# Mixing projection of a hybrid decoder layer: split weights and merged rows through DRAM, row form, first up pair from split units

## The chip, the cores and the metric

One NeuronCore of one Trainium2 chip runs the whole layer in one launch. The metric is the device time in microseconds (us), the median over the runs; one further execution was recorded by the profiler. Engines: TensorE (PE, matmuls), the scalar engine (ACT), the vector engine (DVE), GpSimd (POOL), and SyncE (SP), which here issues every DMA.

## What is computed

The layer takes 1024 prompt tokens and 8 sample tokens (1032 columns in all), width 1024, in float32. Cut to what matters here:

```python
z = x @ w_in                                  # bg, cg, xv, q, k, v, og, ig, fg, ga, gb
ya = (bg * causal_dwconv3(cg * xv)) @ w_proj_a
yb = (sigmoid(og) * MHLN(mlstm(q, k, v))) @ w_proj_b        # 4 heads of 256
merged = sigmoid(ga) * ya + sigmoid(gb) * yb
x = layer_norm(alpha * x + merged @ w_mix_out)              # w_mix_out: 1024 x 1024
ffn = (silu(g) * u) @ w_ffn_down,  [g, u] = causal_dwconv3(x @ w_ffn_up)   # 5632 columns
x = layer_norm(alpha * x + ffn)
```

It also returns the conv and mLSTM states and the rows of the two conv caches.

## The kernel before

Every float32 operand is split into a high and a low part (`split_unit`, `Operands.split`: a cast on ACT, L131 and L159, then a subtraction on DVE, L132 and L160), and each product is three matmuls: high by high, high by low, low by high. Operands of activations stand in SBUF as T00 to T16; split weights rotate through the slots of `WS` (the tiles WS_split, at times also RA and RB); weights are loaded as raw slabs of 1 MB into two halves of `WRB` (WR_raw in the profile).

A `pair` (L186 on) makes 256 output columns for all tokens by seven products instead of eight (combinations of the four quarters of the weight slab, made on DVE in the raw slab and in `XS`, against combinations of operands). `u` = 0 is the first half of the tokens (256 columns a matmul), `u` = 1 the second with the samples (260). Each product is 12 matmuls for each `u`; products go in the order 0 to 6, both `u` after each other, and sums are made by ACT copies into `MC` (L204) and DVE additions (L200).

The order of the program is:

1. Operands of x, then four mLSTM heads (about 140 to 640 us): pairs for K, Q, V, the head's chunks, and gate pairs (`gate_pair`: a pair, a sigmoid on ACT, the rows stored to `sg_d`) as filling, `FILL` = (1,4), (2,5), (3,6), (7,8,9).
2. The conv branch with the decode of the samples beside it (about 640 to 740), drained inside `conv_branch`; gate pair 10 (L666) into RA and RB; `cops`, the conv operands (L743 to L749), by way of `hm_d`; gate pair 11 (L750).
3. Projection A (L763 to L773, about 740 to 813): for each of 8 row blocks a gate row is loaded, 36 matmuls of 344 columns, a DVE product, a store to `ya_d`. After every second block `hidden` (L755 on) loads a piece of the head rows from `hm_d` and makes a piece of the operands `XH`.
4. Four pairs with w_proj_b (L783 to L799): yb times its gate plus ya, the merged row stored to `mg_d`. Rows, gates and ya stand in two sets of tiles in turn.
5. The mix (about 896 to 1000): `merged` loads and splits columns of `mg_d`; `mix` (L801) makes 384 and then 392 token columns, with w_mix loaded and split anew each time; `gemm_rows` (L812) makes the last 256 tokens as rows, with w_mix loaded a third time. `norm1` (L853) transposes the columns back (L863), loads the residual, adds and normalises; `back1` (L872) applies it (L877), transposes (L881), scales (L887) and stores to `x1_d`; `X1` are the operands of the up projection, made by `Operands.first` and `.second`, in which DVE combines (L173 to L179) and splits.
6. 22 up pairs (about 1046 to 1485), the down projection and the last norm.

All is placed on the engines at build time by the framework's scheduler, which fixes the order on each engine; each engine, and SP's queue of DMA issues, works in that order. `tc.issue_after` adds constraints to it.

Of the kernel before, what the change touches and what calls it, by code (L numbers as in the profile page):

```python
# [42 lines left out]
def trunk_kernel(  # L43
# [142 lines left out]
    def pair(w, X, dst, order=nullcontext(), order0=nullcontext()):  # L186
# [28 lines left out]
        with order:  # L215
            vec.tensor_tensor(S3, A11, A21, op=ALU.subtract)  # L216
# [7 lines left out]
            prod(s, 3, qq, True)  # L224
            s = split_unit(S3)
# [7 lines left out]
            vec.tensor_tensor(A12, A12, A11, op=ALU.subtract)  # L233
            s = split_unit(A12)
# [82 lines left out]
    mg_d = dram.tile([8, P, TOK], F32, name="mg_d")  # L317
# [107 lines left out]
    def gate_pair(i, rows):  # L425

        col = (COL_OG, COL_GA, COL_GB)[i // 4] + (i % 4) * 256
        pair(load_pair(w_in[0], col), X, rows_dst(*rows))
# [3 lines left out]
        for j, r in enumerate(rows):  # L432
            sp.dma_start(sg_d[2 * i + j], r)

    def conv_branch(beside):
# [24 lines left out]
        for _ in beside:  # L460
            pass
# [108 lines left out]
    FILL = ((1, 4), (2, 5), (3, 6), (7, 8, 9))  # L570
    for h in range(H):
# [3 lines left out]
        for a, col in ((1, COL_K), (0, COL_Q), (2, COL_V)):  # L575
            pair(load_pair(w_in[0], col + h * 256), X, rows_dst(*qkv[a]))
# [4 lines left out]
        if h == 0:  # L581
# [14 lines left out]
    def decode():  # L596

        vb = Blk("TMF", "dec").v3(0, NS, 256)
# [9 lines left out]
        for h in range(H):  # L608
            if h > 0:
                yield  # L610
# [4 lines left out]
            sp.dma_start(vb, vw_d[h].partition_broadcast(P))  # L615
# [17 lines left out]
            for half in range(2):  # L633
                for c in range(4):
# [89 lines left out]
    MRG = [("T00", "T01", "T02", "T03"), ("T10", "T11", "T12", "T13"), ("T14", "T15")]  # L724

# [5 lines left out]
    def merged(c, stages):  # L731

        n, span = CH[c]
        mg = Many(MRG[c], f"mg{c}", 8, n)
        for i, (k, cnt_) in enumerate(mg.parts(0, 8, 2)):
            blk, base = stages[i % len(stages)]
            a = blk.v3(base, cnt_, n)
            load_cols(a, mg_d[k:k + cnt_], span)
            mg.put(k, a)
        return mg  # L740
# [4 lines left out]
    for k in range(4):  # L745
        r = TS.v(0, TOK)
        sp.dma_start(r, hm_d[8 + k])
        for c, (lo, n) in enumerate(CA):
            cops[c].put(k, r[:, lo:lo + n].unsqueeze(1))  # L749
    gate_pair(11, SG)  # L750

# [370 lines left out]
```

## Time and profile before

| | |
|---|---|
| median of 3 runs | 1761.27 us (1755.98 to 1764.26) |
| profiled execution, its own time | 1759.24 us |
| its span (first to last instruction) | 1757.3 us, mean granted clock 0.982 |
| PE, DVE, ACT, POOL busy | 1693.0, 1234.1, 833.5, 46.8 us |
| chain that ended last | PE 87%, DVE 5%, DMA 5%, ACT 1% |
| moved by DMA | 240.03 MB, mean 137 GB/s |

PE is the engine that the others serve, so the questions are where it does not work, what released it then, and at which clock it worked. The stretches give busy time of each engine in a window and the clock that was granted (PEclk, a share of 2.4 GHz; 0.50 is 1.2 GHz). The waits add up idle time of one engine by what ended it. The chain goes back from the last instruction to whatever released each piece.

### The profile page before, as it was taken

The numbers are of one execution on the slowest core, as the hardware profiler recorded it, in microseconds if no ns is written. First come the engines' busy times: TensorE is split into PE (matmuls) and PEld (weight loads), VectorE is DVE, ScalarE is ACT, GpSimd is POOL, SyncE is SP. The second block draws the span as 40 slices with busy tenths as digits, with TensorE's granted clock in tenths as the row PEclk, the third lists the DMA queues.
The fourth block names the chain that finished last, engine by engine and source line by source line (L and its number), as shares of the span: only waits on it lengthen the run. The fifth ranks groups of instructions, "written<-read, shape, count | busy, mean of one in ns | idle before, by whom it ended". The sixth has DMA issues, their size and how long they took to land.

```text
span 1757.3 us, 32559 instructions
## 1 busy us (share of the span) xinstructions
PE 1693.0 (96%) x12793; PEld 1621.4 (92%) x12793; DVE 1234.1 (70%) x2490; ACT 833.5 (47%) x1640; POOL 46.8 (3%) x97
## 2 busy tenths in 40 slices
PE   8999999999999999997989859999999999999998
PEld 6999999999999999997989749999999999888986
DVE  8867567567477788675764668877888778645675
ACT  7545435345354544442345665544544446433442
POOL 0000001001000000000000000000000000000000
PEclk9999999999999999998999969999999999999999
DMA  4224213224224565586565631332222323845763
GB/s 153 61 83 126 91 61 108 80 67 130 76 76 145 185 204 183 181 276 242 194 224 187 195 100 61 102 104 73 73 73 84 97 74 127 271 144 173 242 210 126
DMA packets 234004, 240.03 MB, mean 137 GB/s; under 512 B 19499, under 2 KB 209979, under 8 KB 233331
## 3 DMA queue, kind: packets, MB, share of 16 engines
q1 hardware_dynamic: 233851, 237.96, 41.9%
q8 instruction: 100, 1.64, 0.4%
q14 instruction: 53, 0.43, 0.1%
HBM read 180.48 MB, written 57.54 MB: 135 GB/s over the span
## 4 chain that ended last, share of the span: by engine, by line
PE 87%; DVE 5%; DMA 5%; ACT 1%; issue 1%; SPq 0%; POOL 0%; DVEq 0%; POOLq 0%; ACTq 0%
PE wp L142 35%; PE wq L142 27%; PE wq L715 2%; PE wq L716 2%; PE wq L717 2%; PE wp L715 2%; PE wp L717 2%; PE wp L716 2%; PE wp L819 2%; PE wq L819 2%; PE pa L540 1%; PE pa L548 1%; DMA MC_copies<-hm_d 1%; PE pa L515 1%; PE pa L646 1%
## 5 line engine op out<-in xcount | busy, mean ns | idle before, releaser
L142 PE MATMUL wp<-T_x,WS_split 128*128 128x260 f32 (+2 forms) x5016 | 668.9, 285 | 4.7 <-ACT T_x L159 3.2
L142 PEld LDWEIGHTS wp<-T_x,WS_split 128*128 128x128 f32 (+1 forms) x5016 | 624.5, 188 | 15.1 <-issue 5.7
L142 PE MATMUL wq<-T_x,WS_split 128*128 128x260 f32 (+3 forms) x3792 | 504.3, 283 | 2.4 <-ACT T_x L159 0.7
L131 ACT CAST WS_split<-WR_raw 128x512 fp32r<-128x512 f32 x486 | 294.6, 612 | 443.6 <-PE wp L142 182.8
L132 DVE TENSOR_TENSOR WS_split<-WR_raw,WS_split 128x512 fp32r<-128x512 f32 x486 | 327.4, 679 | 247.3 <-ACT WS_split L131 243.5
L142 PEld LDWEIGHTS wq<-T_x,WS_split 128*128 128x128 f32 (+1 forms) x3792 | 471.6, 187 | 6.8 <-ACT T_x L159 0.9
L204 ACT COPY MC_copies<-wp 128x256 f32<-128x256 f32 (+1 forms) x336 | 123.8, 369 | 110.3 <-PE wp L142 104.7
L142 PE MATMUL wp<-T_hid,WS_split 128*128 128x260 f32 (+1 forms) x384 | 51.0, 287 | 10.9 <-DVE RA_ga L772 10.9
L132 DVE TENSOR_TENSOR WS_split<-XS_combo,WS_split 128x512 fp32r<-128x512 f32 (+1 forms) x58 | 38.9, 671 | 31.9 <-ACT WS_split L131 31.8
L142 PEld LDWEIGHTS wp<-T_hid,WS_split 128*128 128x128 f32 x384 | 48.6, 193 | 11.4 <-ACT T_hid L159 11.1
L131 ACT CAST WS_split<-XS_combo 128x512 fp32r<-128x512 f32 (+1 forms) x58 | 35.1, 608 | 37.2 <-PE wp L142 37.2
L716 PE MATMUL wp<-T_h,WS_split 128*128 128x512 f32 (+1 forms) x116 | 43.0, 371 | 0.0
L717 PE MATMUL wp<-T_h,WS_split 128*128 128x512 f32 (+1 forms) x116 | 43.0, 370 | 0.0
L715 PE MATMUL wp<-T_h,WS_split 128*128 128x512 f32 (+1 forms) x116 | 42.9, 370 | 0.0
L717 PE MATMUL wq<-T_h,WS_split 128*128 128x512 f32 (+1 forms) x116 | 42.9, 370 | 0.0
L716 PE MATMUL wq<-T_h,WS_split 128*128 128x512 f32 (+1 forms) x116 | 42.9, 369 | 0.0
L715 PE MATMUL wq<-T_h,WS_split 128*128 128x512 f32 (+1 forms) x116 | 42.8, 369 | 0.0
L216 DVE TENSOR_TENSOR XS_combo<-WR_raw 128x512 f32<-128x512 f32 x56 | 38.3, 684 | 1.6 <-DMA WR_raw<-in_w_proj_b_dram 1.0
L218 DVE TENSOR_TENSOR WR_raw<-WR_raw 128x512 f32<-128x512 f32 x56 | 38.5, 688 | 1.2
L842 POOL TENSOR_TENSOR rs<-rs,FX_fixed 128x1 f32<-128x1 f32 (+1 forms) x18 | 12.0, 668 | 1017.5 <-DVE rs L841 1017.5
L142 PE MATMUL wq<-T_hid,WS_split 128*128 128x256 f32 (+1 forms) x288 | 38.8, 287 | 0.0
L217 DVE TENSOR_TENSOR WR_raw<-WR_raw 128x512 f32<-128x512 f32 x56 | 38.3, 683 | 0.3
(528 smaller groups left out, 2628.9 us busy)
## 6 DMA issues: line engine op xcount, KB each, us to landing
WR_raw<-in_w_ffn_down_dram SPq DMA_DIRECT2D x27, 1024.0 KB
WR_raw<-in_w_in_dram SPq DMA_DIRECT2D x26, 1024.0 KB
WR_raw<-in_w_ffn_up_dram SPq DMA_DIRECT2D x44, 512.0 KB
WR_raw<-in_w_mix_out_dram SPq DMA_DIRECT2D x12, 1024.0 KB
sg_d<-RA_sg SPq DMA_DIRECT2D x12, 516.0 KB
sg_d<-RB_sg SPq DMA_DIRECT2D x12, 516.0 KB
WR_raw<-in_w_ffn_down_dram SPq DMA_DIRECT2D x8, 768.0 KB
h_d<-QA_xf SPq DMA_DIRECT2D x11, 516.0 KB
```

The costliest lines, as they stand in the source:

```text
L131: act.copy(wh, w)
L132: vec.tensor_tensor(wl, w, wh.bitcast(F32), op=ALU.subtract)
L142: pe.matmul(ps, a[:, k, :], b[:, k, :], start=start and k == 0 and i == 0, stop=stop and k == kt - 1 and i == 2, skip_group_check=onto)
L204: act.copy(t[u], ps[u][:, :UN[u]])
L216: vec.tensor_tensor(S3, A11, A21, op=ALU.subtract)
L217: vec.tensor_tensor(A21, A21, A22, op=ALU.add)
L218: vec.tensor_tensor(A11, A21, A11, op=ALU.subtract)
L515: pe.matmul(s[:, :L], kr[j][:, cs], qr[j][:, cs], start=(j == 0), stop=(j == 1))
L715: pe.matmul(ps, wh[:, i, :], xh[:, 0, :], start=s, stop=False)
L716: pe.matmul(ps, wh[:, i, :], xl[:, 0, :], start=False, stop=False)
L717: pe.matmul(ps, wl[:, i, :], xh[:, 0, :], start=False, stop=e)
L819: pe.matmul(ps[t][g], a[:, 0, cols], b[:, 0, :], start=s and i == 0, stop=e and i == 2)
```

## The change

- **Splitting ahead.** While heads 1 to 3 run, `presplit` loads w_mix and the first up pair's weights, splits them on ACT and DVE (by way of RA and RB), and stores high and low parts to DRAM (`wm_d`, `wu_d`). Three steps of it stand in each K, Q and V pair (`next(beside)`).
- **Gates and decode.** Gate pair 7 leaves head 3 and comes after gate pair 11, its rows kept in SBUF; gate pair 10 writes to QA and comes before decode is drained. Decode steps are halved.
- **Projection A.** The four pieces of `hidden` come before it; it starts with the blocks 6 and 7, whose ya stay in SBUF.
- **w_pb pairs.** Order 2, 0, 1, 3; one set of gates in QA; the merged rows are split here and both parts are stored.
- **Mix.** The split w_mix is loaded once and stays. Tiles 0 to 3, 6 and 7 of 128 tokens are made as rows (`rows_mm`), tokens 512 to 767 and the samples as columns. Residuals are loaded before they are wanted.
- **First up pair.** `first_pair` takes its seven units from `wu_d`, and goes through products 0 and 1 for both halves, then 2 to 6 for the first half, then for the second.

```diff
@@ pair: the same three steps in each K, Q, V pair of heads 1 to 3
         with order:
+            next(beside, None)
             vec.tensor_tensor(S3, A11, A21, op=ALU.subtract)
...
@@ beside the heads
+    def presplit(jobs):
+        RAW, PRE = Blk("RA", "praw"), Blk("RB", "pre", F32R)
+        def split(w, dsts):
+            h, l = (PRE.v3(i * 512, w.shape[1], w.shape[2]) for i in range(2))
+            act.copy(h, w)
+            vec.tensor_tensor(l, w, h.bitcast(F32), op=ALU.subtract)
+            for d, t in zip(dsts, (h, l)):
+                sp.dma_start(d, t.bitcast(F32))
...
+    JOBS = [()] + [[mix_job(k) for k in range(4)], [mix_job(k) for k in range(4, 8)], [up_job]]
+    FILL = ((1, 4), (2, 5), (3, 6), (8, 9))
@@ conv branch, decode, gates
-    conv_branch(decode())
+    dec = decode()
+    conv_branch(dec)
+    SQ = Blk("QA", "sg")
+    SQ = [SQ.v(i * TOK, TOK) for i in range(2)]
+    gate_pair(10, SQ)
+    for _ in dec:
+        pass
     SG = [Blk(q, "sg").v(0, TOK) for q in ("RA", "RB")]
-    gate_pair(10, SG)
...
+    gate_pair(11, SG, w=wg)
+    gate_pair(7, SG, keep=True)
@@ projection A
+    T5 = Blk("T05", "stage")
+    hidden(1, 0, P, T5.v3(0, 8, P), T5.v3(D, 8, P))
+    for i in range(2):
+        hidden(0, i * P, P, *(WRB.v3(wr[i] + j * D, 8, P) for j in range(2)))
+    hidden(1, P, 132, WRB.v3(wr[1], 8, 132), MC.v3(0, 8, 132))
+    WA = Blk("TMA", "wa").v3(0, 4, 256)
+    for i, m in enumerate((6, 7, 0, 1, 2, 3, 4, 5)):
...
@@ w_pb pairs
+        pair(w, XH, rows_dst(*ys[(i + 1) % 2]))
         for j in range(2):
+            m = 2 * s + j
+            y, g, a = ys[(i + 1) % 2][j], gates[j], YA[j]
+            vec.tensor_tensor(y, y, g.bitcast(F32), op=ALU.mult)
+            vec.tensor_tensor(y, y, a, op=ALU.add)
+            h, l = g, a.bitcast(F32R)
+            act.copy(h, y)
+            vec.tensor_tensor(l, y, h.bitcast(F32), op=ALU.subtract)
+            for k, t in enumerate((h, l)):
+                stored = sp.dma_start(mg_d[k, m], t.bitcast(F32))
@@ mix: split w_mix resident (WM), rows of tokens
+    def rows_mm(t, ps, ks, first, last):
+        for k in ks:
+            xh, xl = (MT[t].v(a * D + k * P, P) for a in range(2))
+            for i, (x, w) in enumerate(((xh, WM[k][0]), (xl, WM[k][0]), (xh, WM[k][1]))):
+                for g in range(2):
+                    pe.matmul(ps[g], x, w[:, g * 512:(g + 1) * 512], start=k == first and i == 0, stop=k == last and i == 2)
...
+    jobs = [lambda k=k: load_wm(k) for k in (2, 3, 4, 5)] + [lambda t=t: load_rows(t, 6, 8) for t in range(3)]
+    jobs += [lambda k=k: load_wm(k) for k in (6, 7)]
...
+    for k in range(6):
+        for t in range(3):
+            rows_mm(t, PS[t], [k], 0, 7)
     for t in range(3):
+        rows_mm(t, PS[t], [6, 7], 0, 7)
...
@@ last tiles, first up pair
+    rows_mm(6, pt[0], range(8), 0, 7)
+    rows_mm(7, pt[1], (2, 3, 7, 5, 6, 1, 0, 4), 2, 4)
...
+    X1[1].first(256, xb[:, :, 0:4])
...
+        for u in range(2):
+            prod(0, u, pp, True)
+            act.copy(m1[u], pp[u][:, :UN[u]])
+            prod(1, u, qa, True)
+            vec.tensor_tensor(dst((0, 0), u), qa[u][:, :UN[u]], m1[u], op=ALU.add)
+        for i in range(2, 7):
+            unit[i] = load_unit(wu_d[i])
+        for u in range(2):
+            ps = pp[u][:, :UN[u]]
+            prod(2, u, pp, False)
...
```

How the change moves instructions is shown at three places. Rows give the line of the kernel they are from, the operation, the tile written and those read, the shape and a count.

**SP, where the conv branch's rows leave QA** (QA_conv holds conv rows; out_dram are the results; TMA_dec, TMB_dec and RB_dec are decode's). Before:

```order
L459 DMA hm_d<-QB_conv 128x1032
L496 DMA hm_d<-ho 128x2x8
L662 DMA out_dram<-RB_dec 8x128
L466 DMA out_dram<-QA_conv 8x128
L468 DMA out_dram<-QA_conv 4x128 x8
L747 DMA TMA_stage<-hm_d 128x1032
L728 DMA WR_raw<-in_w_proj_a_dram 128x4x256
L433 DMA sg_d<-RA_sg 128x1032
L433 DMA sg_d<-RB_sg 128x1032
```

Now:

```order
L464 DMA hm_d<-QB_conv 128x1032
L499 DMA hm_d<-ho 128x2x8
L469 DMA out_dram<-QA_conv 8x128
L471 DMA out_dram<-QA_conv 4x128 x5
L695 DMA out_dram<-RB_dec 8x256
L471 DMA out_dram<-QA_conv 4x128 x3
L711 DMA TMA_dec<-in_state_mlstm_C_dram 128x2x256 x2
L711 DMA TMB_dec<-in_state_mlstm_C_dram 128x2x256 x2
L247 DMA WR_raw<-in_w_in_dram 128x8x256
```

The conv rows' stores out of QA, eight together before, now stand in two lots with a store of decode's rows in between, and decode's state loads follow.

**SP, behind the last w_pb pair** (WS_split, T_wmix, TMF_wmix, QA_rows and RA/RB_wmix are the places of the resident w_mix; T_mg are token tiles of merged rows). Before:

```order
L728 DMA WR_raw<-in_w_mix_out_dram 128x8x256
L799 DMA mg_d<-QA_rows 128x1032
L942 DMA XS_combo<-in_cache_ffn_conv_dram 128x128 x4
L799 DMA mg_d<-QA_rows 128x1032
L705 DMA QB_stage<-mg_d 128x2x384 x2
L728 DMA WR_raw<-in_w_mix_out_dram 128x8x256
L705 DMA QB_stage<-mg_d 128x2x384
L705 DMA T_stage<-mg_d 128x2x384
```

Now:

```order
L984 DMA T_mg<-mg_d 128x6x128 x3
L989 DMA WS_split<-wm_d 128x1024 x4
L989 DMA T_wmix<-wm_d 128x1024 x2
L885 DMA mg_d<-QA_rows 128x1032 x2
L885 DMA mg_d<-RB_rows 128x1032
L885 DMA mg_d<-RA_rows 128x1032
L989 DMA TMF_wmix<-wm_d 128x1024 x2
L984 DMA T_mg<-mg_d 128x2x128 x6
L989 DMA QA_rows<-wm_d 128x1024 x2
L989 DMA RA_wmix<-wm_d 128x1024
L989 DMA RB_wmix<-wm_d 128x1024
```

Two loads of raw w_mix and the columns of merged rows give way to twelve loads of split w_mix, with the last merged rows' stores and their reload in between.

**PE, at the start of the first up pair** (T_x are the operands X1, L142 the products; L881 and L958 are the same transposes of `back1`, L863 those of `norm1`, L943 those of the cache). Before:

```order
L881 MATMUL pa<-FX_fixed,TMA_xres 128x128 x8
L863 MATMUL pa<-FX_fixed,QB_ymix_10869 128x128 x8
L881 MATMUL pa<-FX_fixed,TMB_xres 128x128 x8
L863 MATMUL pa<-FX_fixed,QB_ymix_10869 8x128 x8
L881 MATMUL pa<-FX_fixed,TMA_xres 128x8 x8
L943 MATMUL pa<-FX_fixed,XS_combo 128x128 x5
L943 MATMUL pa<-FX_fixed,XS_combo 128x64
L142 MATMUL wp<-T_x_10756,WS_split 128x256 x12
L142 MATMUL wq<-T_x_10759,WS_split 128x256 x12
L881 MATMUL pa<-FX_fixed,TMA_xres 128x128 x8
L142 MATMUL wp<-T_x_11237,WS_split 128x260
```

Now:

```order
L958 MATMUL pa<-FX_fixed,WR_raw 128x128 x8
L142 MATMUL wp<-T_x_10826,WS_split 128x256 x12
L142 MATMUL wq<-T_x_10829,WS_split 128x256 x12
L142 MATMUL wp<-T_x_11301,WS_split 128x260
L142 MATMUL wq<-T_x_11304,WS_split 128x260
L142 MATMUL wp<-T_x_11301,WS_split 128x260 x11
L142 MATMUL wq<-T_x_11304,WS_split 128x260 x11
L142 MATMUL wp<-T_x_10947,RA_split 128x256 x8
L958 MATMUL pa<-FX_fixed,TMA_xres 128x128 x4
L142 MATMUL wp<-T_x_10947,RA_split 128x256 x2
L958 MATMUL pa<-FX_fixed,TMA_xres 128x128 x4
L142 MATMUL wp<-T_x_10947,RA_split 128x256 x2
```

Transposes of columns and of the cache no longer stand ahead of the products; products 0 and 1 for both halves come first, and the last tile's transposes (TMA_xres) stand inside product 2.

## Rows read from the trace of the kernel before

**Rows 1.** Page, head and part 1: busy time, share of the span, instructions.

```profile
span 1757.3 us, 32559 instructions
...
PE 1693.0 (96%) x12793; PEld 1621.4 (92%) x12793; DVE 1234.1 (70%) x2490; ACT 833.5 (47%) x1640; POOL 46.8 (3%) x97
```

**Rows 2.** Stretches: us, then PE, PEld, DVE, ACT, POOL busy, PEclk, DMA share, GB/s.

```profile
140.00:640.00 500.00, 500.00 (x4113) 490.50 (x4113) 334.85 (x863) 233.10 (x502) 27.72 (x58) 1.00 0.34 109
...
740.00:830.00 90.00, 77.85 (x531) 76.37 (x531) 60.01 (x109) 35.18 (x65) 0.00 (x0) 0.92 0.78 264
...
896.00:1046.00 150.00, 117.01 (x637) 108.81 (x635) 90.11 (x161) 85.19 (x178) 5.50 (x8) 0.86 0.56 172
1046.00:1485.00 439.00, 436.84 (x3630) 435.69 (x3631) 356.50 (x631) 223.85 (x410) 0.85 (x1) 1.00 0.27 84
```

**Rows 3.** PE's waits: line, what for, us in total, times, longest us.

```profile
PE pa L881 <- ACT TMA_xres L877: 13.0, 2, 7.9
PE wp L142 <- DVE RA_ga L772: 10.9, 1, 10.9
PE wq L715 <- ACT RA_split L131: 7.5, 1, 7.5
PE pa L881 <- ACT TMB_xres L877: 5.1, 1, 5.1
...
PE pa L943 <- DMA XS_combo<-in_cache_ffn_conv_dram: 3.8, 1, 3.8
```

**Rows 4.** Chain of waits, 780 to 830: start us, us, what.

```profile
796.54 0.43 SPq L792
...
797.53 10.21 DMA MC_copies<-hm_d
...
813.53 2.90 PE wp L142 x12
...
818.85 2.85 PE wp L142 x24
```

**Rows 5.** Chain of waits, 890 to 912.

```profile
898.90 4.22 DMA T_stage<-mg_d
...
906.82 2.87 DMA mg_d<-RA_rows
```

**Rows 6.** Chain of waits, 1000 to 1072.

```profile
1002.52 6.62 DMA x_d<-T_xf
...
1030.95 4.56 DMA TMA_xres<-in_x_prompt_dram
```

**Rows 7.** Stretches around the idle time of rows 3, columns as in rows 2.

```profile
800.00:820.00 20.00, 9.14 (x54) 8.89 (x53) 11.47 (x20) 5.79 (x10) 0.00 (x0) 0.66 1.01 386
...
910.00:920.00 10.00, 9.56 (x45) 9.56 (x46) 4.67 (x7) 4.61 (x8) 0.00 (x0) 0.79 0.74 236
...
1010.00:1020.00 10.00, 3.68 (x16) 3.28 (x16) 7.44 (x15) 7.07 (x16) 1.45 (x2) 0.50 0.19 57
1020.00:1030.00 10.00, 4.09 (x20) 3.01 (x20) 4.15 (x9) 6.72 (x14) 0.54 (x1) 0.50 0.39 109
1030.00:1040.00 10.00, 6.08 (x28) 5.22 (x28) 4.78 (x13) 3.33 (x13) 0.55 (x1) 0.50 0.60 168
1040.00:1050.00 10.00, 6.09 (x36) 5.60 (x36) 10.00 (x23) 8.47 (x20) 0.85 (x1) 0.84 0.25 71
```

**Rows 8.** Page, part 5: busy us, mean ns, then the idle time before.

```profile
L131 ACT CAST WS_split<-WR_raw 128x512 fp32r<-128x512 f32 x486 | 294.6, 612 | 443.6 <-PE wp L142 182.8
L132 DVE TENSOR_TENSOR WS_split<-WR_raw,WS_split 128x512 fp32r<-128x512 f32 x486 | 327.4, 679 | 247.3 <-ACT WS_split L131 243.5
```

**Rows 9.** Chain of waits, 936 to 942 and 1700 to 1757: matmuls and transposes.

```profile
935.85 0.17 PE wq L715
...
939.51 0.76 PE pa L863 x7
...
1738.48 2.79 PE wp L819 x12
```

More of the change, by code (lines that the diff above doesn't have):

```diff
@@ L614, in decode @@
             sp.dma_start(vw_d[h], vw)
-            sp.dma_start(vb, vw_d[h].partition_broadcast(P))
+        for h in range(H):
             b = bank()
@@ L729, in load_slab, with load_unit @@
         return t
[L731 to L740, printed above, removed]
+    def load_unit(src):
+        blk, base = WS[cnt["unit"] % len(WS)]
+        cnt["unit"] += 1
+        sp.dma_start(blk.v(base, 1024).bitcast(F32), src)
+        return blk.v3(base, 4, P), blk.v3(base + 512, 4, P)
     cops = [Many(q, f"conv{c}", 4, 344) for c, q in enumerate((("QA",), ("QB",), ("TMF", "TMB")))]
     TS = Blk("TMA", "stage")
[L745 to L750, printed above, removed]
+    wg = load_pair(w_in[0], COL_GB + 768)
+    with tc.issue_after(cnt["slab"].ins):
+        for k in range(4):
+            r = TS.v(0, TOK)
+            sp.dma_start(r, hm_d[8 + k])
+            for c, (lo, n) in enumerate(CA):
+                cops[c].put(k, r[:, lo:lo + n].unsqueeze(1))
+    gate_pair(11, SG, w=wg)
+    gate_pair(7, SG, keep=True)
     XH = [Operands(u, "hid") for u in range(2)]
@@ L784, in trunk_kernel @@
[L784 to L789 removed]
+        if i < 6:
+            sp.dma_start(ya_d[m], row)
+    RQ = [Blk(q, "rows", F32R) for q in ("QA", "QB")]
+    gates = [RQ[0].v(i * TOK, TOK) for i in range(2)]
+    RY = [Blk(q, "rows") for q in ("TMF", "TMA", "TMB")]
@@ new lines, in two @@
+    def two(pool_=None):
+        return [bank() for _ in range(2)] if pool_ else [wbank(q) for q in ("wp", "wq")]
+    for k in range(2):
+        load_wm(k)
+    xr = [residual(t, t) for t in range(2)]
+    for t, tag in ((0, "T12"), (1, "T13"), (2, "T10")):
+        MT[t] = Blk(tag, "mg", F32R)
+        load_rows(t, 0, 6)
+    jobs = [lambda k=k: load_wm(k) for k in (2, 3, 4, 5)] + [lambda t=t: load_rows(t, 6, 8) for t in range(3)]
+    jobs += [lambda k=k: load_wm(k) for k in (6, 7)]
+    for i, job in enumerate(jobs):
+        with tc.issue_after(last_rows[0].ins if i < 3 else stored.ins if i == 3 else queued.ins):
+            queued = job()
@@ new lines, in trunk_kernel @@
+    for t, tag in ((6, "T12"), (7, "T13")):
+        MT[t] = Blk(tag, "mg", F32R)
+        load_rows(t, 0, 8)
+    ns = [norm1(None, 0, t, xr[t], PS[t]) for t in range(3)]
+    XF10 = Blk("T10", "xf")
+    xfs = [tile_dst(MC), XF10.v3(0, 8, P), XF10.v3(D, 8, P)]
+    for t in range(3):
+        back1(ns[t], xfs[t], t * P)
+        if t < 2:
+            X1[0].first(t * P, xfs[t])
+    PS = two()
+    rows_mm(3, PS, range(8), 0, 7)
+    n3 = norm1(None, 0, 3, xr[3], PS)
+    xfs.append(Blk("T11", "xf").v3(0, 8, P))
@@ new lines, in trunk_kernel @@
+    X1[0].second(0, xfs[0], xfs[2])
+    back1(n3, xfs[3], 3 * P)
+    X1[0].second(P, xfs[1], xfs[3])
+    YM, YMS = WRB.v3(cnt["raw"] % 2 * 2048, 8, 256), XS.v3(0, 8, NS)
+    for m in range(8):
+        ps = next_bank()
+        n = MCH[0]
+        for k in range(8):
+            xh, xl = mgf.at(k)
+            wh, wl = (w[:, m * P:(m + 1) * P] for w in WM[k])
+            for i, (w, x) in enumerate(((wh, xh), (wh, xl), (wl, xh))):
+                pe.matmul(ps[:, :n], w, x[:, 0, :], start=k == 0 and i == 0, stop=k == 7 and i == 2)
+        act.copy(YM[:, m, :], ps[:, :256])
+        act.copy(YMS[:, m, :], ps[:, 256:n])
@@ L931, in trunk_kernel @@
+    WS += [(Blk(q, "split", F32R), 0) for q in ("RA", "RB")]
     Y2 = Blk("QB", "ymix2")
```

288 lines of the change are left out of this document (170 added, 118 removed).

## The prediction, made before the changed kernel ran

> **What bounds the kernel now.** I read the page's first part, then the stretches, the waits of TensorE (PE), the chain of waits, and the granted clock. PE is busy 1693.0 us of the span of 1757.3 [rows 1], so what can be won is where it idles, where its clock is down, and what it does without need. The stretches show where it idles [rows 2]: 140–640 (the four heads) is full, 500.00 of 500.00; 740–830 (projection A) lacks 90.00 − 77.85 = 12.15 us, 896–1046 (the mix and norm 1) lacks 32.99, 1046–1485 (the up pairs) lacks 2.16. Together **47.3 us**.
>
> The waits name what PE stood for [rows 3]: 10.9 us at the first w_pb pair, behind the vector engine's (DVE) row product of projection A; 7.5 at the start of the mix; 13.0 and 5.1 at the transposes of norm 1 (in three waits); 3.8 for cache rows. The chain says why. Before the first w_pb pair it is a load of stored head rows that took 10.21 us [rows 4]; its operands and then the row product follow on DVE, and PE goes on at 813.53. At the mix it is a round trip through DRAM: merged rows loaded in 4.22 us, the last merged row stored in 2.87, and behind it the cast of a w_mix unit [rows 3, 5]. In norm 1 it is a store of 6.62 us that holds DVE, and a residual load of 4.56 [rows 6].
>
> The clock is the second loss. Where the clock is granted at 0.50 throughout, PE was busy 3.68, 4.09 and 6.08 us [rows 7]; at 2.4 GHz that is half as much, so 6.9 us were lost. At 0.66 over 20 us, 13.6 us ran at 1.2 GHz, and the matmuls in them are those from 813.53 on, about 5 us to 818.5: 2.5 lost [rows 4, 7]. At 0.79 over 10 us, 4.2 us ran low, busy nearly all: 1.9. At 0.84 likewise 3.2 us: 1.6. Every one comes directly after an idle stretch. Sum **12.9 us**.
>
> **The change part by part.** (1) *Idle and clock.* The edits aim at each of these waits: head rows are staged before the projection, w_mix comes split from DRAM and stays, residuals are loaded early, the first up pair comes split. I take all of the idle and the low clock away, −47.3 − 12.9 = **−60.2**, and then charge what is late next.
>
> (2) *PE's own work.* The row form of tiles 0–3 spares the 32 transposes at L863 of tiles 0 to 3 (8 each): seven took 0.76 us [rows 9], 0.109 each, so **−3.5**. The mix keeps 480 matmuls: before 192 of 384, 192 of 392 and 96 of 512 columns, now 288 of 512 and 192 of 264, the same 198,144 columns. A 512 takes 2.79/12 = 0.233 us, a 384 takes 0.17 [rows 9], a 256 or 260 takes 2.85/24 = 0.119 [rows 4]. With these, about 90 us on both sides; I book +0.7 for the form of 264.
>
> (3) *Splitting ahead in heads 1–3.* 23 scalar-engine (ACT) casts at 612 ns and 23 DVE subtractions at 679 [rows 8] are 14.1 and 15.6 us, four combinations 2.7 more; 46 stores of 256 KB and 13 loads, about 17 MB. ACT has 233.10 and DVE 334.85 busy of 500, DMA a share of 0.34 at 109 GB/s [rows 2]; 17 MB over some 375 us add 45 GB/s. I charge nothing: PE covers it. The same casts and subtractions leave the mix, and ACT and DVE were what PE waited for there. If the cover fails, see the second rival. The eight added casts and subtractions on merged rows lie under pairs of 168 × 0.119 = 20 us: nothing.
>
> (4) *Gate pair 10 into QA.* Its first DVE result has to wait for the conv branch's small stores out of QA. The excerpt on SyncE (SP) has them behind the second conv row's store, among them a store of decode's rows: some ten issues at 0.43 us [rows 4], then a landing of about 3 [rows 5]. Those are 7 to 8 us; with the conv rows' last DVE work in the pair's first 5 us, that is some 13 us behind its start, and PE can run to about 11.5 (product 4 is put ahead of 3, so 96 matmuls at 0.119). Charged **2** (0 to 5, at which the store would take as long as in rows 6).
>
> (5) *Decode in half steps, projection after `hidden`.* Gates 11 and 7 and the four staged pieces now stand between the conv branch and the projection, so PE has two pairs (40 us) more to cover the loads of the head rows. No row shows the new wait; bounds 0 and 5 (half of the old 10.9, which needed one load of 10.21). Nearer to the lower end, since loads have 40 us: **1**.
>
> (6) *w_pb pairs with one set of gates.* Gates of the next pair reload into QA only after the split rows have left it. Weights, gates, rows, stores and the first w_mix rows are 23 MB in 80 us, 294 GB/s; the trace has 264 over 90 us and 386 over 20 [rows 2, 7]. PE itself writes to other rows, in two sets; it is held only when DVE, which works in order, stands at a gate. **0.5** (0 to 10: one more wait like 10.9).
>
> (7) *Last pair to mix.* The excerpt has, behind the last pair, 12 loads of split weights of 512 KB, 4 stores and 6 small loads: 9.2 MB. PE starts from what is resident (k of 0 and 1, three tiles); one k takes 18 × 0.233 = 4.2 us, so k of 2 is wanted at 8.4, k of 6 at 25, k of 7 at 29.4. That asks for 313 GB/s, inside the 264 to 386. **1** (0 to 9.4, the old 7.5 with its 1.9 of clock).
>
> Here the Trainium skill speaks against the change: "DMA: Bandwidth & Descriptors", section Bandwidth, wants transfers of 1 MiB or more for three quarters of the peak, and gives about 358 GB/s of HBM as a core's limit. Pieces of 512 KB would then stay under 268 GB/s, an estimate from that page: 9.2 MB take 34 us, PE waits some 5 for k of 7, and the sum comes out as in rival (a). The trace of before does not bear the rule out: 386 GB/s was moved in pieces of about this size [rows 7].
>
> (8) *First up pair.* The last tile's norm (statistics, two activations, eight transposes) now lies behind both first products, and five products of each half of the tokens follow as the operands come. The old opening cost 10.00 − 6.09 = 3.9 idle [rows 7], at most 2.2 behind it [rows 2] and 1.6 of clock, 7.7 in all. The excerpt shows why it does not go to zero: only 48 matmuls of 0.119 and the transposes stand between the last row matmul and products that need tile 7, and u = 1 needs four columns of tile 6 at once. DVE makes the operands at 0.6 to 0.7 us each. **5.5** (2 to 12).
>
> Sum: 1759.24 − 60.2 − 3.5 + 0.7 + 2 + 1 + 0.5 + 1 + 5.5 = 1706.2 on the profiled execution, which lies 2.0 below the median 1761.27. Forecast **1708 us**, −3.0%. All lower ends (2 in all) give 1700; all upper ends (41.4) 1740.
>
> **The rivals.** *(a) The DMA engines become the bound.* At 264 GB/s [rows 2] the 9.2 MB take 34.8 us, k of 7 is 5.4 late, and the low clock follows as in rows 7 (1.9); the 23 MB of the pairs take 87 us instead of 80. That is 14, less the 1.5 booked under (6) and (7): 1721. For: a share of 0.78 over 90 us at 264 GB/s. Against: 386 GB/s over 20 us. The page of the Trainium skill named above stands on this side.
>
> *(b) Slower: the splitting ahead stalls ACT in the heads.* Each of the 23 jobs casts into one buffer (RB), whose two stores must have landed; ACT works in order, and behind a held cast stand the copies out of PSUM and the weight casts that PE needs. Jobs come three to a pair, 6.7 us apart. Cast, subtraction and store together take 0.6 + 0.7 us and the landing. With 2.87 [rows 5] that fits; with 6.62 [rows 6] it is 1.2 over, at most 28 in all; with 10.21, as the load of [rows 4], it is 4.8 over, 110 in all: 1818. It makes the kernel slower from 53/23 = 2.3 us a job, a landing of 7.7. Against: 10.21 was seen at a DMA share near 1, here it is 0.34.
>
> *(c) The wait at projection A moves instead of going.* Stores of conv and decode now share SP's queue with the weights of gate 11, and DVE's operand work comes in one block under gate 7; if a load of 10.21 us [rows 4] is late there, 10.9 and 2.5 of clock come back: 1708 + 12 = 1720.
>
> *(d) The change does not do what it says.* The round trips stay, only through other tiles (merged rows of the last pair, tile 7's norm), and half of PE's idle and clock comes back at least; 1708 + 30 to 50: 1738 to 1758, at the upper end no change.
>
> **How the numbers follow.** Forecast 0.57 (1698 to 1716), (a) 0.18 (1716 to 1733), (c) 0.11 (1716 to 1726), (d) 0.09 (0.05 of it within 0.5% of before, the rest faster), (b) 0.05. A difference of 0.5%, 8.8 us, is about what a measurement of this kernel can tell from none. The range holds the first three, 0.86, less what lies past their edges: **1697 to 1733**. Faster 0.57 + 0.18 + 0.11 + 0.04 = 0.90; same 0.05; slower 0.05.
>
> **What would show it.** Right: in the heads PE still full; from projection A to norm 1 no PE wait over 2 us; granted clock 1.00 there; ten to fifteen us idle left, most of it at the first up pair. Wrong: PE waiting for a load of w_mix or of merged rows in the mix (a); any idle between 280 and 640, with ACT standing at DMA (b); a wait on DVE or on a load of head rows at the projection or the first w_pb pair (c); a span above 1738 (d).

## The result and the profile after

The changed kernel takes **1713.61 us** (median of 4 runs, 1711.82 to 1716.12) against 1761.14 before: ratio 0.9734, 95% interval 0.9707 to 0.9761. The forecast was 1708 with a range of 1697 to 1733. Run once more beside three experiments it gave 1715.67 (1714.74 to 1718.74). The profiled execution took 1716.12, the slowest of the first four. Head, part 1 and the stretches of its profile (columns as in [rows 2]):

```profile
span 1714.3 us, 32475 instructions
...
PE 1673.6 (98%) x12761; PEld 1596.0 (93%) x12761; DVE 1207.1 (70%) x2453; ACT 808.2 (47%) x1603; POOL 50.2 (3%) x97
```

```profile
140.00:640.00 500.00, 493.31 (x4054) 482.01 (x4054) 348.02 (x886) 237.65 (x515) 30.31 (x58) 1.00 0.45 143
640.00:740.00 100.00, 96.47 (x826) 91.44 (x825) 74.65 (x161) 48.26 (x96) 4.53 (x3) 1.00 0.59 189
740.00:810.00 70.00, 67.46 (x471) 66.72 (x470) 52.37 (x96) 33.70 (x62) 0.00 (x0) 1.00 0.63 197
810.00:890.00 80.00, 77.36 (x640) 77.16 (x640) 55.69 (x84) 30.93 (x61) 0.00 (x0) 0.98 0.68 246
890.00:1000.00 110.00, 106.65 (x606) 91.56 (x605) 47.79 (x93) 44.26 (x106) 4.39 (x8) 0.98 0.79 252
1000.00:1440.00 440.00, 434.64 (x3632) 432.58 (x3632) 354.07 (x632) 226.50 (x420) 0.55 (x1) 1.00 0.28 88
```

Two things are to be seen against [rows 2]. The mix, 150 us long with 33.0 idle, is a stretch of 110 with 3.4 idle. And the heads, full before, now lack 6.7 us of 500. What PE waited for (columns as in [rows 3]):

```profile
PE pa L269 <- DMA QA_x<-in_x_prompt_dram: 4.4, 1, 4.4
PE wp L142 <- ACT MC_copies L204: 4.0, 7, 1.4
PE wp L997 <- DMA T_mg<-mg_d: 3.3, 2, 3.2
PE wp L142 <- DVE RB_sg L857: 2.6, 1, 2.6
PE wp L142 <- ACT T_x L159: 2.6, 1, 2.6
PE wq L142 <- DVE QA_qkv L200: 2.5, 3, 1.2
PE wp L142 <- ACT QA_qkv L234: 2.4, 1, 2.4
PE wq L142 <- DVE QA_sg L200: 1.6, 1, 1.6
...
PE wp L142 <- DVE RA_sg L857: 1.4, 1, 1.4
```

The waits of 7 to 13 us in [rows 3] are gone; behind the program's start (QA_x) the longest is 3.2. QA_qkv (L234, L200) is in the heads, RB_sg and RA_sg are the end of projection A, T_mg the start of the mix, T_x the first up pair, QA_sg gate pair 10; MC_copies stands in several stages. While PE works, the clock (columns as above) is low in four short stretches instead of the long ones of [rows 7]:

```profile
325.00:335.00 10.00, 7.62 (x52) 7.41 (x51) 5.50 (x11) 4.24 (x9) 0.00 (x0) 0.83 0.47 169
810.00:820.00 10.00, 7.36 (x50) 7.16 (x50) 5.16 (x11) 1.59 (x4) 0.00 (x0) 0.83 0.89 324
895.00:905.00 10.00, 6.80 (x22) 5.13 (x23) 5.50 (x5) 2.11 (x2) 0.00 (x0) 0.83 1.10 361
1000.00:1010.00 10.00, 7.16 (x46) 6.75 (x46) 5.23 (x15) 8.32 (x23) 0.55 (x1) 0.83 1.02 268
```

0.83 over 10 us is 3.4 us at 1.2 GHz, with PE busy: 1.7 lost in each, 6.8 in all.

From the starts and ends of the matmuls in the trace, the stages last (us). Heads: first matmul of a pair to the last products with head 3's values; conv: to the first matmul of projection A; projection A: to the first w_pb pair; pairs: to the mix; mix: to the first up product; up: to the last up product; rest: to PE's end.

| | heads | conv, gates | proj. A | w_pb pairs | mix | up | rest |
|---|---|---|---|---|---|---|---|
| before | 533.5 | 198.0 | 64.0 | 83.0 | 139.9 | 458.6 | 254.6 |
| changed | 540.4 | 198.0 | 53.1 | 84.2 | 105.7 | 453.7 | 253.6 |
| difference | +6.9 | 0.0 | −10.9 | +1.2 | −34.2 | −4.9 | −1.0 |

The sum, −42.9, is the difference of the spans, −43.0. So the gain was where the sum had put it, and its loss is in the heads, where the sum had charged nothing. The 0.0 of the stage with the gates hides two changes: new waits of some 4.4 us, and decode's 128 matmuls (L646 before, L720 now), which keep PE busy for 11.28 us instead of 14.80.

Pieces of the chain of waits tell how the new waits arose. In head 1:

```profile
318.76 8.27 DMA RA_praw<-in_w_mix_out_dram
...
327.62 0.61 ACT WS_split L131
328.24 0.28 ACT QA_qkv L234
...
328.56 2.13 PE wp L142 x12
```

A raw row of w_mix took 8.27 us to land; ACT stood at its cast, and the copy out of PSUM and the weight cast that PE needed were queued behind. In head 3, where the first up pair's weights are split, it was DVE that stood:

```profile
446.60 7.17 DMA RA_praw<-in_w_ffn_up_dram
...
453.80 0.04 DVE RA_praw L622
...
454.41 0.15 DVE QA_qkv L200
...
458.34 3.97 DMA wu_d<-RB_pre
...
463.69 0.35 DVE QA_qkv L200
```

Once it stood at a raw load and once at a store out of the buffer RB, each time with an addition (L200) behind it that PE waited for. At the end of projection A:

```profile
791.15 7.14 DMA ya_d<-RB_sg
...
798.31 4.59 DMA RB_sg<-sg_d
802.92 1.36 DVE RB_sg L857 x3
...
804.63 5.49 DMA ya_d<-RB_sg
...
810.14 3.69 DMA RB_sg<-sg_d
```

A row is stored and the next gate loaded through one tile, in turn. At the mix:

```profile
888.37 2.80 SPq L874
...
891.69 7.10 DMA T_mg<-mg_d
```

SP's queue stood at the load of ya for the last pair, and the merged rows that the mix begins with were issued behind it.

### The profile page after: what moved, and what is told of

Its sections match the earlier page's. It is cut to its first block, busy times and chain, and to the rows that moved or that the text cites. A ratio compares the mean times of both kernels' runs of the same rounds, so it can differ in the third digit from the quotient of the medians.

```text
span 1714.3 us, 32475 instructions
## 1 busy us (share of the span) xinstructions
PE 1673.6 (98%) x12761; PEld 1596.0 (93%) x12761; DVE 1207.1 (70%) x2453; ACT 808.2 (47%) x1603; POOL 50.2 (3%) x97
## 4 chain that ended last, share of the span: by engine, by line
PE 82%; DMA 9%; DVE 4%; ACT 3%; issue 1%; SPq 0%; POOL 0%; DVEq 0%; ACTq 0%; POOLq 0%
PE wp L142 33%; PE wq L142 24%; PE wp L794 2%; PE wq L795 2%; PE wp L796 2%; PE wq L796 2%; PE wq L794 2%; PE wp L795 2%; PE wq L894 2%; PE wp L894 2%; DMA RA_praw<-in_w_mix_out_dram 1%; PE wp L997 1%; PE pa L543 1%; PE wq L997 1%; PE pa L551 1%
## 5 line engine op out<-in xcount | busy, mean ns | idle before, releaser
L142 PE MATMUL wp<-T_x,WS_split 128*128 128x260 f32 (+2 forms) x5016 | 664.5, 283 | 10.9 <-ACT MC_copies L204 4.0
L142 PEld LDWEIGHTS wp<-T_x,WS_split 128*128 128x128 f32 (+1 forms) x5016 | 619.8, 188 | 21.3 <-ACT MC_copies L204 6.7
L142 PE MATMUL wq<-T_x,WS_split 128*128 128x260 f32 (+3 forms) x3792 | 503.7, 282 | 6.8 <-DVE QA_qkv L200 2.5
L142 PEld LDWEIGHTS wq<-T_x,WS_split 128*128 128x128 f32 (+1 forms) x3792 | 470.0, 187 | 11.7 <-DVE QA_qkv L200 3.1
L131 ACT CAST WS_split<-WR_raw 128x512 fp32r<-128x512 f32 (+1 forms) x444 | 269.4, 611 | 370.5 <-PE wp L142 155.9
L132 DVE TENSOR_TENSOR WS_split<-WR_raw,WS_split 128x512 fp32r<-128x512 f32 (+1 forms) x444 | 298.1, 676 | 179.7 <-ACT WS_split L131 175.7
L204 ACT COPY MC_copies<-wp 128x256 f32<-128x256 f32 x330 | 121.5, 369 | 84.6 <-PE wp L142 81.1
L142 PE MATMUL wp<-T_hid,WS_split 128*128 128x256 f32 (+1 forms) x384 | 50.6, 286 | 4.0 <-DVE RB_sg L857 2.6
L142 PEld LDWEIGHTS wp<-T_hid,WS_split 128*128 128x128 f32 x384 | 48.2, 193 | 4.5 <-DVE RB_sg L857 2.8
L796 PE MATMUL wp<-T_h,WS_split 128*128 128x512 f32 (+1 forms) x116 | 42.9, 370 | 0.0
L795 PE MATMUL wp<-T_h,WS_split 128*128 128x512 f32 (+1 forms) x116 | 42.9, 370 | 0.0
L580 DVE TENSOR_TENSOR RB_pre<-RA_praw,RB_pre 128x512 fp32r<-128x512 f32 x23 | 15.9, 692 | 36.9 <-ACT RB_pre L579 24.1
L492 POOL TENSOR_TENSOR t<-t,FX_fixed 128x1 f32<-128x1 f32 (+1 forms) x36 | 26.8, 744 | 464.1 <-DVE t L491 455.6
L579 ACT CAST RB_pre<-RA_praw 128x512 fp32r<-128x512 f32 x23 | 14.3, 620 | 53.7 <-DMA RA_praw<-in_w_mix_out_dram 27.6
```

Of the source, the lines that this page charges most:

```text
L131: act.copy(wh, w)
L132: vec.tensor_tensor(wl, w, wh.bitcast(F32), op=ALU.subtract)
L142: pe.matmul(ps, a[:, k, :], b[:, k, :], start=start and k == 0 and i == 0, stop=stop and k == kt - 1 and i == 2, skip_group_check=onto)
L204: act.copy(t[u], ps[u][:, :UN[u]])
L492: pool.tensor_tensor(t[:rows], t[:rows], nh[:rows], op=ALU.pow)
L795: pe.matmul(ps, wh[:, i, :], xl[:, 0, :], start=False, stop=False)
```

## The experiments

Each is an edit of the changed kernel unless said otherwise. Single runs of one kernel lie 3 to 9 us apart, so edits worth 2 to 5 us are read from the stages of the trace first.

**The projection part alone.** The kernel before, with the changed kernel's code from `gate_pair` and `decode` to the end of projection A, all ya stored:

```diff
-    FILL = ((1, 4), (2, 5), (3, 6), (7, 8, 9))
+    FILL = ((1, 4), (2, 5), (3, 6), (8, 9))
...
+    gate_pair(11, SG, w=wg)
+    gate_pair(7, SG, keep=True)
```

> The kernel before with only the part between the conv branch and the w_pb pairs taken over: gate pair 7 behind gate pair 11 with its rows kept, gate pair 10 into QA ahead of decode's rest, decode in half steps, the four pieces of hidden ahead of projection A, blocks 6 and 7 first. Theory (each stage's idle was its own, so the parts add up): from the heads' end to the first w_pb pair it took 254.9 us before and 243.8 in the changed kernel, so this part alone gives 11 us, about 1750 against 1761; the mix keeps its waits of 7.5, 13.0 and 5.1. Rival (the time won ahead of the mix is lost again at the mix, where w_mix loads and the merged rows then meet earlier): under 5 us, 1756 or more, with the longer wait at the start of the mix.

Measured: 1742.95 us, 16.6 less than the kernel before beside it (ratio 0.9909, 0.9894 to 0.9923). Projection A lasts 52.6 us. The mix keeps its waits:

```profile
PE pa L892 <- ACT TMA_xres L888: 12.0, 2, 6.8
PE wq L721 <- ACT RA_split L131: 6.8, 1, 6.8
PE pa L892 <- ACT TMB_xres L888: 5.1, 1, 5.1
```

The rival is out: nothing won ahead of the mix is lost there. The theory's 11 us were too few: projection A gives 11.4, and beside it the heads last 530.2, 3.3 less than before, and up is 2.0 shorter, for which no run here has a cause.

**One split row only.**

```diff
-    JOBS = [()] + [[mix_job(k) for k in range(4)], [mix_job(k) for k in range(4, 8)], [up_job]]
+    JOBS = [(), [mix_job(0)], (), ()]
-            i = sp.dma_start(WM[k][a].bitcast(F32), wm_d[k, a])
+            i = sp.dma_start(WM[k][a].bitcast(F32), wm_d[0, a])
```

> The changed kernel, which splits ahead only four rows of w_mix in head 1 and nothing in heads 2 and 3; every load of split weights in the mix and in the first up pair reads the first split row instead (the results of mix and FFN are left out by that), with the same sizes and counts of loads there. Theory (the heads lost 7.1 us to the splitting, 2.4 and the clock of 1.7 in head 1 and 2.7 in head 3): idle in head 3 goes, head 1 keeps its stall, 3 us less than 1713.6. Rival (the stalls are head work that other changes of order cause, or the heads' stores to DRAM are not to blame): idle between 440 and 470 us stays and the time is 1713 or more.

By the code, one row in head 1 is split (the text says four), so the theory's stall in head 1 was not put to the test. Measured: 1709.90 us (1705.44 to 1714.46); heads 531.6, 7 to 9 less than the changed kernel's two profiles (540.4 and 538.3). PE in the heads:

```profile
140.00:640.00 500.00, 497.54 (x4122) 487.76 (x4121) 340.30 (x877) 234.52 (x506) 33.32 (x59) 1.00 0.37 116
```

The stalls of heads 1 and 3 are both gone, so the splitting is their cause; by the length of the heads it costs **7 to 9 us**. Waits make about 4 of that (2.5 us without PE in this stretch against 6.7 and 6.3 in the changed kernel's two profiles) and the low clock 1.7 in one of the two. In the rest, some 3 us, PE is busy, only longer; its cause is open.

**Raw rows by halves, loaded two steps ahead.**

```diff
+            load(0)
+            load(1)
+            for n, (k, g) in enumerate(hs):
+                yield
+                split(raw[n % 2], ...)
+                if n + 2 < 8:
+                    load(n + 2)
```

> The changed kernel; the splitting of w_mix in heads 1 and 2 loads half rows of 256 KB into the two halves of the raw buffer in turn, two steps ahead, instead of whole rows into one buffer one step ahead. Theory (ACT, in order, stood 7.14 us at the cast of a raw row whose load took 8.27, and behind it the copy out of PSUM): ACT's waits for RA_praw (27.6 us in 8) nearly go, the 2.4 us of PE at 326 and the low clock behind it go, 4 us less: 1709.5. Rival (the stores of the split halves hold it, or the DMA volume): ACT's waits only move to the store, PE still stalls 2 us or more in head 1, time within 1 us of 1713.6.

A miss: 1719.71 us, heads 539.9. The wait for w_mix left ACT's list of waits at this cast and came back as another. In the changed kernel:

```profile
ACT RB_pre L579 <- DMA RA_praw<-in_w_mix_out_dram: 27.6, 8, 7.1
ACT RB_pre L579 <- DMA wm_d<-RB_pre: 8.7, 8, 1.3
```

With halves:

```profile
ACT RB_pre L579 <- DMA wm_d<-RB_pre: 28.2, 14, 4.5
```

Now the stores of the previous piece out of the one buffer RB hold the cast, which is what the prediction's rival (b) had named. Why the median is 6 us longer stays open: the profiled execution, 1717.50, is 1.4 to 2.3 above the changed kernel's two, and it lasts 2.0 longer behind the up pairs, in work that the edit does not touch.

**Gate rows and ya by thirds.**

```diff
-            sp.dma_start(row, sg_d[8 + m])
+            for lo, n in CA:
+                sp.dma_start(row[:, lo:lo + n], sg_d[8 + m][:, lo:lo + n])
```

(and the store of ya likewise, behind each product)

> The changed kernel; in projection A the gate row is loaded and ya stored in three pieces of 344 columns instead of whole rows of 1032, in the same two tiles RA and RB. Theory (the end of the projection is bound by the round trip store, land, load through one tile: 7.14 + 4.59 and 5.49 + 3.69 us against 11.3 us of matmuls for two rows, so PE waited 0.33, 1.35 and 2.64 and then ran 3.4 us at the low clock): with pieces the trip begins a third or two earlier, the three waits go or fall under 1 us together, 3 to 6 us less, 1708 to 1711. Rival (the DMA engines, or SP's queue, are the limit there: share 0.77 at 780 to 820, and 28 more issues): waits stay or grow, 1713 or more.

Measured: 1715.22 us (1710.93 to 1717.29), no gain by the runs. In the trace the waits behind the projection fell from 4.3 us to 1.1 and 1.4, not under 1 together as the theory had it, the clock stayed up there, and projection A and pairs together last 133.8 us (137.3 and 136.3 in the changed kernel's two profiles). This execution lost 3 us at the program's start, ahead of all edits, where its clock was 0.66 and the changed kernel's 1.00:

```profile
15.00:25.00 10.00, 8.62 (x52) 5.92 (x50) 9.93 (x19) 9.77 (x24) 0.00 (x0) 0.66 0.55 175
```

**The mix's first rows ahead of ya.**

```diff
         pair(w, XH, rows_dst(*ys[(i + 1) % 2]))
+        if i == 3:
+            for t, tag in ((0, "T12"), (1, "T13"), (2, "T10")):
+                MT[t] = Blk(tag, "mg", F32R)
+                load_rows(t, 0, 6)
+            with tc.issue_after(last_rows[0].ins):
+                for j in range(2):
+                    sp.dma_start(YA[j], ya_d[2 * s + j])
```

> The changed kernel; for the last w_pb pair the two loads of ya are issued behind the six loads of merged rows that the mix begins with, instead of between them. Theory (PE's wait of 3.19 us at the start of the mix is one of order on SP: its queue stood 2.80 us at the load of ya until a store out of the same tile had landed, and the loads of rows behind it came so much later): the wait falls under 0.5 us and the low clock of 3.4 us behind it goes (1.7), 3 to 5 us less, 1709 to 1711, unless the last pair's merge now comes late by what ya lands later. Rival (the DMA engines are the limit there, share 1.03 at 880 to 900, 1.01 and 1.08 behind): the loads land at the same time, the wait stays at 2.5 us or more.

Measured: 1715.33 us (1710.25 to 1716.74). The wait of 3.2 falls to 0.6, about as the theory had it, and the clock stays at 1.00 to 999 us; the mix lasts 102.9 instead of 105.7:

```profile
PE wp L1004 <- DMA T_mg<-mg_d: 0.8, 2, 0.6
PE wp L1004 <- issue: 0.7, 1, 0.7
```

So the order on SP set this wait, not the DMA engines' rate; the median alone does not show the gain.

**The first up pair as an ordinary pair.**

```diff
-            first_pair(rows_dst(gr, ur))
+            pair(load_pair(w_up[0], j * P, FF + j * P), X1, rows_dst(gr, ur), tc.issue_after(ns[0][4].ins))
```

(with `[up_job]` taken out of JOBS)

> The changed kernel with the first up pair as an ordinary pair, its weights loaded raw and split in place (as in the kernel before, with the transposes of the cache behind it), and without the splitting ahead in head 3 that served it. Theory (the first up pair by halves gains little: 5 us of waits and a low clock of 1.7 stand there where before it was 6 and 1.6, and its splitting costs 2.7 us in head 3): head 3's stalls go, the opening costs 2 to 6 us more, together within 3 us of 1713.6. Rival (the halves are what keeps PE busy while the last tile's norm runs): 6 us or more slower, with a wait on an operand of 5 us or more at the opening.

Measured: 1715.69 us (1714.36 to 1717.35). Up lasts 2.2 us longer, the stalls in head 3 are gone. As the theory had it: the halves gain about what their splitting costs.

**Thirds and rows first together, and both with the ordinary pair.** The edits above, combined.

> Both edits together: ya and gate rows of projection A by thirds, and the mix's first rows ahead of the last ya loads. In the run with thirds alone the three waits at the end of the projection went from 4.3 to 2.5 us and the low clock there went, though its median was not lower. Theory (stalls at different stages add): waits at the end of the projection 2.5, at the mix under 0.5, no low clock at either, 6 to 8 us less than the changed kernel, 1706 to 1708. Rival (what is won in one stage comes back as a wait in the next): over 1711.

> The same two edits, with the first up pair as an ordinary pair and nothing split ahead in head 3. Theory: equal to the kernel with the two edits within 3 us, as the pair alone. Rival: 6 us or more slower than it, as the halves keep PE busy.

Measured: 1709.15 us (1706.67 to 1712.87; ratio 0.9716, 0.9696 to 0.9736), and with the ordinary pair **1703.13** (1700.94 to 1705.68; 0.9676, 0.9658 to 0.9694). The first is 1 us above the theory's range, with no wait over 0.7 us at either stage and the clock up at both. The second is 6 us under it, more than the 3 expected, and the pair alone did not give that. Its heads last 535.3 instead of 539.4, its up 455.4 instead of 453.4; but the profiled executions of the two, 1706.67 and 1705.68, are only 1 us apart, so the stages do not tell where the 6 come from.

**Residuals late.** Tiles 0 to 3 share two residual tiles, those of tiles 2 and 3:

```diff
-    xr = [residual(t, t) for t in range(2)]
+    xr = [residual(t, 2 + t) for t in range(2)]
...
-        xr += [residual(t, t) for t in (2, 3)]
```

> The changed kernel; the residual rows of the token tiles 0 to 3 share two tiles, as in the kernel before, so those of tiles 2 and 3 are loaded only when the norm of tiles 0 and 1 is through. Theory (norm 1 left PE's path because the matmuls of other tokens now stand behind each norm, 11 us for tile 3 and 23 for the columns, and not because of the early loads): PE waits nowhere more than now, within 3 us of the changed kernel. Rival (the loads of 4.56 us and the store that held DVE for 6.62 were what PE waited for, and taking them out early made the gain): waits at the transposes of tiles 2 and 3 come back with 5 us or more, and the low clock behind them, 8 us or more slower.

> The changed kernel itself once more, on the same chip as the next two, since single runs of it differ by 4 us and the edits are worth 2 to 8. All theories: 1711 to 1717.

Measured: 1720.34 us (1717.75 to 1722.42) against the 1715.67 of the changed kernel beside it. No wait at the transposes of tiles 2 and 3: there the order covers the norm, as the theory had it. One of 4.9 us came at the last tile, which neither had. The chain of waits and PE's waits show it:

```profile
997.43 9.06 DMA x_d<-MC_copies
...
1006.52 1.89 ACT MC_copies L964 x6
```

```profile
PE pa L958 <- ACT TMA_xres L954: 4.9, 1, 4.9
```

ACT stood for a store of a token tile out of MC before it could write the next tile there, and the last tile's norm was behind it. So the 18.1 us of waits in norm 1 went by the order of the work. The early loads are worth some 3 to 5 us, less than the rival's 8: the median is 4.7 longer, but the stages from the w_pb pairs to up only 3.5 (647.2 against 643.6), and the heads, ahead of the edit, are longer too. Part of the 3.5 is not norm 1: SP stood 3.56 and 2.60 us at the last pair's two ya loads (2.80 and 0.43 in the changed kernel), and the stage of the pairs is 1.8 us longer. The changed kernel has the same store (8.64 us) ahead of its 2.6 us wait for T_x at the first up pair.

**Splitting spread over three heads.** To the version of 1703.13:

```diff
+            yield
             for g in range(2):
...
+    JOBS = [()] + [[mix_job(k) for k in range(3)], [mix_job(k) for k in range(3, 6)], [mix_job(k) for k in range(6, 8)]]
```

> The version with ya by thirds, the mix's first rows ahead and the ordinary first pair (1703.1 when last run, 5 us under the same with the first pair by halves), with the splitting of w_mix spread over heads 1 to 3 (three rows, three, two instead of four, four, none) and one step more between a raw load and its cast. Theory (what the splitting costs the heads is ACT standing at a raw load of up to 8.27 us that is one step old): ACT's waits for raw rows fall from some 25 us to under 10, PE's wait of 2.8 at 326 goes, the heads take 2 to 4 us less, 1699 to 1702. Rival (as when the rows were loaded by halves: the wait moves to the stores of the split halves): heads no shorter, 1703 or more.

A miss: 1706.99 us (1704.60 to 1709.15), heads 539.7, the wait of 2.6 at 326 still there and one of 2.5 more in head 3. The scheduler put the casts where they had been, so ACT's wait for raw rows was 30.3 us, against 30.2 without the edit. The theory was not tested by it.

**The cast behind what PE needs.** To the version of 1703.13:

```diff
             for u in range(2):
-                act.copy(dst((1, 0), u), pp[u][:, :UN[u]])
+                cnt["out"] = act.copy(dst((1, 0), u), pp[u][:, :UN[u]])
             vec.tensor_tensor(A12, A12, A11, op=ALU.subtract)
-            next(beside, None)
             s = split_unit(A12)
+            next(beside, None)
...
+            with tc.issue_after(cnt["cast"].ins), tc.issue_after(cnt.get("out", cnt["cast"]).ins):
+                act.copy(h, w)
```

(`cnt["cast"]` is the last weight cast)

> The version with ya by thirds, the mix's first rows ahead and the ordinary first pair (1703.1 when run, heads' end 535.3 us behind the first matmul of a pair, PE's wait of 2.76 at 326), with one change in the heads: on ACT the cast of a raw w_mix piece stands behind the second copy out of PSUM and the last weight cast of the pair, not ahead of them. The loads and stores stay as they were. Theory (what the splitting costs the heads is the order on ACT: the copy and the cast that PE needs stood behind a cast whose load took 8 us): ACT still waits some 7 us at the raw row, PE's wait of 2.76 goes or falls under 1, the heads are 2 to 4 us shorter than 535.3 at the same granted clock, 1699 to 1702. Rival (PE has too little work ahead wherever the cast stands, 24 matmuls of 0.119 in the next product): the wait moves to the next weight cast, heads no shorter, 1703 or more.

Measured: 1703.21 us (1701.61 to 1704.66; ratio 0.9683, 0.9665 to 0.9700). ACT (start, us, and in brackets its idle time before) and PE in the heads:

```profile
322.18 0.62 ACT L131 CAST WS_split<-WR_raw 128x512 fp32r<-128x512 f32 x1 [2.79 <-PE wp L142]
322.70 0.37 ACT L234 COPY QA_qkv<-wp 128x260 f32<-128x260 f32 x1
326.50 0.62 ACT L580 CAST RB_pre<-RA_praw 128x512 fp32r<-128x512 f32 x1 [3.44 <-issue]
```

```profile
140.00:640.00 500.00, 497.44 (x4113) 487.00 (x4112) 347.38 (x890) 239.50 (x518) 31.85 (x59) 1.00 0.44 137
```

The copy no longer stands behind the cast, the wait of 2.76 is gone, and the heads last 532.6, 2.7 less, with the same loads and stores of the splitting. (ACT waits 14.3 us for raw rows instead of 30.2, at most 4.6 at once, since it asks for them later; the theory had some 7.) So head 1's wait was the order on ACT. That rests on the wait: the heads of one kernel vary by 2 us, as the changed kernel's 540.4 and 538.3. Head 3's loss, at DVE, was not tested by this, since nothing is split there in this version. The median shows no gain: it is equal to the 1703.13, and its profiled execution, 1701.61, was the fastest of five. Both versions beat the changed kernel by more than the intervals are wide.

## Why the prediction was right, and which terms were off

The forecast of 1708 lay 5.6 us low, in the range. Its frame held: PE bounds the kernel, idle and low clock were the gain, and what one stage gains is not lost in the next (shown by the projection part alone). Its terms make, by stage, 0 for the heads, +3.0 for conv and gates, −14.15 for projection A and the w_pb pairs, −41.85 for mix and up, and 0 for the rest; measured were +6.9, 0.0, −9.7, −39.1 and −1.0. On the profiled execution 1706.2 was forecast and 1716.12 came, and the heads are the largest part of these 9.9 us. Its first three signs of being right failed: PE was not full in the heads, waits of more than 2 us stood between projection A and the mix, and the clock fell there. Step by step:

- **(1), (2), projection A to up:** the stages fall short by 4.5 and 2.8 us. At the end of projection A a store and a load in turn through one tile keep 4.3 us of waits, with 1.7 of clock behind them, for which the sum has no term.
- **(3) Splitting ahead, charged 0: this is the term that failed.** The heads cost 7 to 9 us (one split row only). The busy times were about right, DVE 348.0 and ACT 237.7 of 500, but a free engine is no cover if it works in order and stands at a load: rival (b)'s mechanism at a sixth to an eighth of the 53 us from which it decides, mostly at the raw load ahead of the store, in head 3 at the store too. Its sign, idle between 280 and 640 with ACT standing at DMA, came, though the kernel was not slower.
- **(4) Gate pair 10:** 2 charged, 1.6 measured, but the nearness is luck. The chain ahead of this wait (below) has no store of conv rows in it. PE had run out; a cast on ACT, a split on DVE and only then the addition into QA followed. The wait is 1.65 us in all thirteen profiles of kernels with this pair, which landing times would hardly give. Why the addition stands behind the split in DVE's order is not shown.
- **(5) Decode, projection after `hidden`:** 1 charged, 0.9 measured in gate pair 7. A further wait of 1.4 in gate pair 11 has no term: ACT stood 3.0 us at the load of a conv row, behind the rows of gate pair 10, whose store out of QA took 8.73. Decode's shorter matmuls, 3.5 us that the sum did not have either, made up for both.
- **(6) w_pb pairs:** 0.5 charged, no wait inside the pairs; the stage is 1.2 us longer by the wait of 2.6 that projection A leaves at the first of them.
- **(7) Last pair to mix:** 1 charged, 3.2 and 1.7 of clock measured. It was not rate, as rival (a) had it: no wait for w_mix came, and DMA moved 361 GB/s at 895 to 905; it was SP's order (rows first). The prediction's 268 GB/s was worked out wrongly. In the Trainium skill's "DMA: Bandwidth & Descriptors", section Bandwidth, the three quarters are of a peak of 436 GB/s, and the 358 are a core's share with both cores of a pair at work; pieces of less than 1 MiB would then stay under 327 GB/s, an estimate from that page. By that 9.2 MB take 28 us and k of 7 is in time, so the page does not stand on rival (a)'s side. The trace's 361 GB/s, with loads and stores of mostly half a MB, are above the 327 too.
- **(8) First up pair:** 5.5 charged; 5.4 of waits from 1002 to 1029 and 1.7 of clock measured. The size was about right, the cause only in part: ahead of the largest, 2.6, is the store out of MC.
- **The clock:** charged at nothing outside (8), it cost 5.1 more at three waits of 2.4 to 3.2 us.

The chain at gate pair 10:

```profile
707.49 0.62 ACT WS_split L131
...
708.14 0.06 DVE WS_split L132
...
708.75 0.43 DVE QA_sg L200
```

Rival (c)'s sign came, waits on DVE at the end of the projection and the first w_pb pair (4.3 of 13 us), but not its cause: the chain there holds gate rows that came through one tile in turn, and no load of head rows. (d) did not come.

## What to carry to other kernels

Work moved under a busy engine is free only if the engines that do it don't stand still in order: ask what each added instruction waits for, and which work that the bound engine needs is queued behind it. Read short waits from the stages of the trace, since the runs' spread hides them one by one; two such edits and the ordinary first pair together gave 10 us here. A wait for a load can be a place in the issuing queue and not a matter of rate. And a term that comes out near its number is not yet right: look at what stood ahead of the wait.

## What the runs showed of the hardware

The length of a wait does not tell whether the clock falls behind it. At the same place in head 1 a wait of 1.7 us was followed by the low clock in the run with the residuals late, and one of 2.8 us in the version of 1703.13 was not (325 to 335 in both, in this order; 0.86 is 2.8 of the 10 us at 1.2 GHz):

```profile
325.00:335.00 10.00, 8.26 (x58) 8.05 (x58) 4.12 (x8) 3.71 (x8) 0.00 (x0) 0.86 0.65 240
```

```profile
325.00:335.00 10.00, 7.24 (x61) 7.04 (x61) 6.25 (x12) 4.24 (x9) 0.00 (x0) 1.00 0.52 183
```

The wait of 3.2 us at the start of the mix was followed by the low clock in all six profiles that have it. So what a short wait costs in clock differs between executions of like kernels.

The load of 512 KB in head 1 took 8.27 us at a DMA share of 0.73 around it (319 to 327), the 4.56 of [rows 6] stand at a share of 1.00 (1030 to 1036): the lighter share did not make it shorter. A slab of 1 MB had been issued 1.2 us ahead of the longer one; that this was the reason is not shown.
